# Two MLPs of a decoder trunk: the order of up-projection units and down-projection pairs

## Chip, core and metric

The kernel runs on one core of one Trainium2 chip. The metric is the device time of one execution in microseconds (us); lower is better. Three timed runs of the kernel before gave 1999.71, 2004.2 and 1998.16 us.

## What is computed

A decoder trunk of two layers over 256 positions, width 2048, all in float32. Layer 0 mixes with a gated short convolution, layer 1 with multi-head latent attention. Each is followed by an MLP with hidden width 8192, and every sub-layer by a post-norm. The change touches the two MLPs alone:

```python
def sq_relu_mlp(x, w1, w2):
    return jnp.square(jax.nn.relu(x @ w1)) @ w2

h = layer_norm(ALPHA * h + mix, ln_g[layer, 0], ln_b[layer, 0])
h = layer_norm(ALPHA * h + sq_relu_mlp(h, mlp_w1[layer], mlp_w2[layer]), ...)
```

w1 is 2048 x 8192 and w2 is 8192 x 2048 for each layer.

## The kernel before, in words

**Precision.** TensorE multiplies in a reduced float32 form. So each operand is split into a high part (a cast on ScalarE, L127) and the rest, the low part (a subtraction on VectorE, L128). A product is then three matmuls: high x high, high x low and low x high.

**Passes.** An MLP is done in NQ = 8 passes q over the hidden width. A pass makes QC = 8 hidden tiles of 128 columns and multiplies them at once with their rows of w2. Passes 1 to 6 are called FAST.

**Units.** One hidden tile is one unit of W1 (`products`, L288, calling `mm_run`, L221). A unit goes over 16 K tiles. For each it issues a matmul of 512 columns (`high`, L215: the weights' high part against x, high and low side by side) and one of 256 columns (`low`, L219). In the K tile numbered TURNED = 2 of the first unit of a pass the low matmul comes ahead of the high one: the tile is "turned". The sums go to one of four PSUM banks in turn. ScalarE copies half of them out (L355), VectorE adds the other half (L356), and ScalarE applies relu and square (L718, L719). Two hidden tiles make a pair; the pair is split and four sums and differences of its quarters are formed (`form`, L703).

**Products in pairs.** In a FAST pass the 2048 output columns are two groups g of 1024. Each group takes the four pairs j in turn. A "fast" pair (`fast_products`, L343) uses seven products for what needs eight, 21 matmuls of 512 columns (`dot`, L297), and seven PSUM sums named 1 to 7. Its weights come as two tiles of w2f, from which VectorE and ScalarE make the third and fourth matrix (`prepare`, L141). A "plain" pair uses eight products on four sums, 24 matmuls. Group 1 has three fast pairs and a plain one (MIXED = "sssp"), group 0 four fast ones. One matmul of the plain pair is split in two halves (EVEN, L654).

**Sums.** The sums of a pass are kept in SBUF: four in the output's own place `acc`, four extra ones in `sums`. At the end of a group they are copied back (`put_back`, L616) or added (`keep`, L624). Before the next pass's products they are copied into PSUM again (`resumed`, L612), for group 1 during the units of that pass. In the last pass `fold` (L669) combines the extra sums into `acc`.

**Order.** Everything follows the order in which the code is written and the order that the framework's scheduler gives each engine from it. In a FAST pass it is: eight units; four pairs of group 1; four pairs of group 0. Weights are taken from one list, `stream` (L78 to L99), in that order. `take` (L183) prepares a fixed number of steps ahead (LOOK = 5); five raw tiles (L62) and eight pairs of high and low tiles (L63) limit it. Loads are issued on SP (L138).

**Around it.** In the second MLP the residual is transposed on TensorE into `acc` during passes 1 to 4 (`extra`, L1024). In the first MLP chunks of the next norm are prepared in the last pass (`begin`, L798). In the last pass of the second MLP, sums are put into PSUM ahead of the output (`last_sum`, L681).

Of the kernel before, what the change touches and what calls it, by code (L numbers as in the profile page):

```python
# [16 lines left out]
P = 128  # L17
# [20 lines left out]
MIXED = "sssp"  # L38
EVEN = (QC - 1, "22")
# [14 lines left out]
def trunk(ctx: ExitStack, tc: tile.TileContext, xT, vecs, lead, w_first, w_in, w_out, w_kv, w_q, w_uk, w_uv,  # L54
# [27 lines left out]

    def mlp_stream(l):
        out = []
        for q in range(NQ):
            out += halves(w1[l, q * QC:(q + 1) * QC])
            if q not in FAST:
                out += halves(w2[l, q])
                continue
            for j, kind in enumerate(MIXED):  # L90
                out += [(w2f[l, q, 1, j, 0], w2f[l, q, 1, j, 1])] if kind == "s" else \
                    halves(w2[l, q, 2, j]) + halves(w2[l, q, 3, j])
            out += [(w2f[l, q, 0, j, 0], w2f[l, q, 0, j, 1]) for j in range(QC // 2)]
        return out
# [480 lines left out]
    def mlp(idx, ln, blocks, fast, begin=None, extra=None, last=False):  # L575
# [32 lines left out]
        def resumed(p, g, name, bank):  # L608

            ps = psum(name, bank)  # L610
            if q != FAST[0] or p not in OWN:
                nc.scalar.copy(ps, place(p, g))  # L612
            return ps

# [3 lines left out]
        def keep(p, g, ps):  # L618

            at = place(p, g)  # L620
            if q == FAST[0] and p in OWN:
                nc.scalar.copy(at, ps)
            else:
                nc.vector.tensor_tensor(at, at, ps, ALU.add)  # L624

        def resume(busy, free, ps, m):

            b2, b3, b4, b6 = free
            b1, b5, b7, b22 = busy
            for p, bank in {3: (("3", b3),), 4: (("2", b2),), 5: (("4", b4), ("1", b1)), 6: (("6", b6), ("5", b5)),  # L630
                            7: (("7", b7), ("22", b22))}.get(m, ()):
                ps[p] = resumed(p, 1, f"ps_r{p}", bank)

        def down_pairs(h, forms, busy, free, ps):

            b2, b3, b4, b6 = free
            b1, b5, b7, b22 = busy
            new = set(OWN) if q == FAST[0] else set()
            onto = set(ps) - new
            for j, kind in enumerate(MIXED):  # L640
                if kind == "s":
                    last = j == MIXED.rindex("s")
                    fast_products(ps, h, forms, j, new if j == 0 else (), OWN if last else (), onto)
                    if last:
                        for p in OWN:
                            put_back(p, 1, ps[p])
                        then = {p: resumed(p, 0, f"ps_f{p}", bank) for p, bank in (("3", b1), ("1", b5))}
                    continue
                for two in (((0, "2"), (1, "4")), ((1, "22"), (0, "3"))):
                    w, = take(1, LOOK + 1)  # L650
                    for t, p in two:
                        for kk in range(2):
                            k = 2 * j + kk
                            dot(ps[p], wide_rows(w, kk), held(h[k], t), False, k == QC - 1, (k, p) == EVEN, True)  # L654
                    if j == len(MIXED) - 1:
                        if "5" not in then:
                            then.update({p: resumed(p, 0, f"ps_f{p}", bank) for p, bank in (("5", b7), ("7", b6))})
                        for _, p in two:
                            put_back(p, 1, ps[p])
            n = QC // 2  # L660
            onto = set(then) - new
            then.update({p: psum(f"ps_f{p}", bank) for p, bank in (("2", b2), ("6", b4), ("4", b22))})
            for j in range(n):
                fast_products(then, h, forms, j, set(then) - onto if j == 0 else (), then if j == n - 1 else (), onto)
            for p, _, _ in FACTORS:
                (put_back if p in onto or p in new else keep)(p, 0, then[p])
            return (b3, b1, b5, b7), (b6, b2, b4, b22)

        def fold():  # L669

            s1, s5, s7, s6 = (sums[:, i] for i in range(4))
            c = acc.rearrange("p t (g b c) -> p t b g c", g=2, b=2)
            for d, a, b in ((c[:, 0, 0], c[:, 0, 0], s1), (s6, s6, s1), (c[:, 0, 1], c[:, 0, 1], s6), (s7, s7, s6),
                            (c[:, 1, 0], c[:, 1, 0], s7), (c[:, 1, 1], c[:, 1, 1], s7),
                            (c[:, 0, 1], c[:, 0, 1], s5), (c[:, 1, 1], c[:, 1, 1], s5)):
                nc.vector.tensor_tensor(d, a, b, ALU.add)
                yield
# [8 lines left out]
        busy, free = (0, 1, 2, 3), (4, 5, 6, 7)  # L686
        for q in range(NQ):
            ht = act.tile([P, QC, 2 * T], F32R, tag="c", name=f"h{idx}_{q}")
            h = [ht[:, k, :] for k in range(QC)]
            forms = None  # L690
            if q in FAST:
                forms = act.tile([P, QC // 2, 2, 4 * P], F32R, tag="a2", name=f"forms{idx}_{q}")
            pair = []

            def pair_tile(m):

                if m % 2 == 0:
                    pool = (act, "ab") if m % 4 else (fast, "fp")
                    t = pool[0].tile([P, 2 * T], F32, tag=pool[1], name="fp")
                    pair.append(t.rearrange("p (i t) -> p i t", i=2))  # L700
                return pair[-1]

            def form(j):  # L703
                (a11, a21), (a12, a22) = ((pair[j][:, i, :P], pair[j][:, i, P:]) for i in range(2))
                sf = fast.tile([P, 4, P], F32, tag="sf", name="sf")
                s1, s2, s3, s4 = (sf[:, i, :] for i in range(4))
                nc.vector.tensor_tensor(s1, a21, a22, ALU.add)
                nc.vector.tensor_tensor(s3, a21, a11, ALU.subtract)
                nc.vector.tensor_tensor(s2, s1, a11, ALU.subtract)
                nc.vector.tensor_tensor(s4, a12, s2, ALU.subtract)  # L710
                split(forms[:, j, 0, :], forms[:, j, 1, :], sf.rearrange("p i c -> p (i c)"))

            def hidden(m, ps, evac, *func):
                both = pair_tile(m) if q in FAST else None
                f = both[:, m % 2, :] if both is not None else tmp.tile([P, T], F32, tag="fh", name="fh", bufs=3)
                evac(ps, f, *func)
                if not func:
                    nc.scalar.activation(f, f, AF.Relu)  # L718
                nc.scalar.activation(f, f, AF.Square)  # L719
                if both is None:  # L720
                    put_split(h[m], f)
                elif m % 2:
                    at = ht[:, m - 1:m + 1, :]
                    split(at[:, :, :T], at[:, :, T:], both)
                    form(m // 2)

            if q == 0:
                for m in range(QC):
                    if m < GROUP:
                        if m == 0:  # L730
                            ws = ln.ws if ln.ws else group_of(GROUP)
                            if not ln.ws:
                                mm_wide(ws, ln.xd)
                            ln.finish()
                        ps = ws[m][1]
                    else:
                        ws = [(take(), psum("ps_w"))]
                        mm_wide(ws, ln.xd)
                        ps = ws[0][1]
                    hidden(m, ps, ln.weighted, AF.Relu)  # L740
                acc = act.tile([P, 2, D], F32, tag="a1", name=f"acc{idx}")
            else:
                folds = fold()
                begun = {}
                for m, ps in enumerate(products(QC, xhl, TURNED, busy)):
                    hidden(m, ps, whole)
                    if extra and m == 0 and q <= NB:
                        for t in range(2):
                            extra(block, q - 1, t, busy[2 + t])
                    if q in FAST:  # L750
                        resume(busy, free, begun, m)
                    if q == NQ - 1:
                        next(folds, None)
                        if last and m >= QC - 2:
                            for t in range(2):
                                last_sum(m - QC + 2, t, free[2 * (m - QC + 2) + t])
# [19 lines left out]
    def to_wide(block, put, h):  # L776
# [411 lines left out]
```

## Time and profile before

| what | value |
|---|---|
| timed runs, median (lowest to highest) | 1999.71 us (1998.16 to 2004.2) |
| span of the profiled execution, first to last instruction | 1994.9 us |
| from that span to the median of the timed runs | 4.8 us |
| VectorE's full-size split L128, count and mean | 710 of 1220 ns |
| ScalarE's full-size cast L127, count and mean | 710 of 1051 ns |
| HBM read | 381.78 MB, 192 GB/s over the span |

The profile is one execution on the chip; beside its span the page gives no device time of its own. Engines are PE (TensorE matmuls), PEld (TensorE's weight loads), DVE (VectorE), ACT (ScalarE), POOL (GpSimd) and SP. A row of grouped instructions reads: line, engine, operation, out<-in, shapes, count | busy us, mean ns | idle time before them and what ended it. A row of the timeline reads: start in us, duration in us, engine, line, operation. A matmul's duration reaches into the next one, so its cost is read from start to start. A row of the waits reads: who waited for whom, us in total, times, longest.

### The profile page before, as it was taken

How to read it: one execution, taken by the hardware profiler on the slowest of the kernel's cores; microseconds unless marked ns; L12 is line 12 of the kernel's file. 1: busy time of each engine (PE TensorE's matmuls, PEld its weight loads, DVE VectorE, ACT ScalarE, POOL GpSimd, SP SyncE). 2: the span in 40 equal slices, each digit the busy share in tenths (PEclk: the TensorE clock that was granted, in tenths of full speed). 3: DMA queues.
4: the chain of work that ended last, by engine and by line, in shares of the span. 5: the costliest groups of instructions: out<-in, count | busy, mean ns of one | idle time of the engine just before them, and what ended most of it. 6: DMA issues, size and time to landing. Idle time of an engine off the chain costs nothing.

```text
span 1994.9 us, 30180 instructions
## 1 busy us (share of the span) xinstructions
PE 1987.7 (100%) x11110; PEld 1737.2 (87%) x11110; DVE 1709.4 (86%) x2555; ACT 1354.9 (68%) x2154; POOL 2.3 (0%) x21
## 2 busy tenths in 40 slices
PE   9999999999999999999999999999999999999998
PEld 8888888988888888888889998898888888888886
DVE  8667667797999989989978988777899999999985
ACT  6444445586778778777756755558677787887772
POOL 0000000000000000000000000000000000000000
PEclk9999999999999999999999999999999999999999
DMA  8666666565657466574855543656464656656483
GB/s 318 205 191 187 190 190 190 179 193 157 212 170 251 148 216 221 177 243 147 281 171 159 170 140 123 201 180 195 146 233 155 232 161 220 222 178 233 150 269 130
DMA packets 106853, 385.85 MB, mean 193 GB/s; under 512 B 11857, under 2 KB 12625, under 8 KB 106449
## 3 DMA queue, kind: packets, MB, share of 16 engines
q1 hardware_dynamic: 106560, 383.79, 59.5%
q8 instruction: 87, 1.43, 0.3%
q14 instruction: 62, 0.50, 0.1%
q10 hardware_dynamic: 144, 0.13, 0.0%
HBM read 381.78 MB, written 2.10 MB: 192 GB/s over the span
## 4 chain that ended last, share of the span: by engine, by line
PE 98%; DVE 1%; ACT 1%; issue 0%; DVEq 0%; ACTq 0%
PE ps_u L215 20%; PE ps_l L215 13%; PE ps_u L219 10%; PE ps_l L219 7%; PE ps_f L300 4%; PE ps_f L303 4%; PE ps_f L302 4%; PE ps_r L303 4%; PE ps_r L302 4%; PE ps_r L300 4%; PE ps_d L300 2%; PE ps_d L302 2%; PE ps_d L303 2%; PE ps_w L249 2%; PE ps_w L248 2%; PE ps_w L247 2%
## 5 line engine op out<-in xcount | busy, mean ns | idle before, releaser
L128 DVE TENSOR_TENSOR lo<-raw,hi 128x1024 fp32r<-128x1024 f32 x710 | 861.8, 1220 | 190.6 <-ACT hi L127 119.9
L127 ACT CAST hi<-raw 128x1024 fp32r<-128x1024 f32 x710 | 741.8, 1051 | 247.4 <-PE ps_l L215 98.1
L215 PE MATMUL ps_u<-xhl,hi 128*128 128x512 f32 x1792 | 621.7, 392 | 0.0
L219 PE MATMUL ps_u<-xhl,lo 128*128 128x256 f32 x1792 | 498.2, 279 | 0.0
L215 PEld LDWEIGHTS ps_u<-xhl,hi 128*128 128x128 f32 x1792 | 334.5, 187 | 73.6 <-ACT acc L595 0.2
L219 PEld LDWEIGHTS ps_u<-xhl,lo 128*128 128x128 f32 x1792 | 338.1, 189 | 1.8
L215 PE MATMUL ps_l<-xhl_a,hi 128*128 128x512 f32 x704 | 244.1, 393 | 0.0
L219 PE MATMUL ps_l<-xhl_a,lo 128*128 128x256 f32 x704 | 195.4, 279 | 0.0
L215 PEld LDWEIGHTS ps_l<-xhl_a,hi 128*128 128x128 f32 x704 | 132.1, 188 | 29.9
L219 PEld LDWEIGHTS ps_l<-xhl_a,lo 128*128 128x128 f32 x704 | 131.9, 188 | 0.2
L127 ACT CAST hi_t<-raw_t 128x1024 fp32r<-128x1024 f32 x84 | 88.5, 1054 | 45.8 <-DVE raw_t L162 41.4
L162 DVE TENSOR_TENSOR raw_t<-raw,raw 128x1024 f32<-128x1024 f32 x84 | 102.3, 1218 | 1.8 <-DMA raw<-in_w2f_dram 1.5
L128 DVE TENSOR_TENSOR lo_t<-raw_t,hi_t 128x1024 fp32r<-128x1024 f32 x84 | 102.4, 1219 | 0.2
L718 ACT ACTIVATE fp<-fp 128x256 f32<-128x256 f32 x96 | 40.0, 416 | 63.2 <-DVE fp L356 62.6
L215 PE MATMUL ps_l<-z,hi 128*128 128x512 f32 x240 | 82.4, 391 | 0.0
L300 PE MATMUL ps_d<-hi,h 128*128 128x512 f32 x192 | 75.0, 391 | 0.0
L302 PE MATMUL ps_d<-lo,h 128*128 128x512 f32 x192 | 75.0, 390 | 0.0
L303 PE MATMUL ps_d<-hi,h 128*128 128x512 f32 x192 | 74.8, 389 | 0.0
L249 PE MATMUL ps_w<-xd,hi 128*128 128x258 f32 x256 | 72.7, 284 | 0.0
L248 PE MATMUL ps_w<-xd,lo 128*128 128x258 f32 x256 | 72.3, 282 | 0.0
L247 PE MATMUL ps_w<-xd,hi 128*128 128x258 f32 x256 | 72.3, 282 | 0.0
L215 PE MATMUL ps_l<-oT,hi 128*128 128x512 f32 x208 | 71.3, 391 | 0.0
(296 smaller groups left out, 3963.7 us busy)
## 6 DMA issues: line engine op xcount, KB each, us to landing
raw<-in_w_dram SPq DMA_DIRECT2D x344, 512.0 KB, 4.5
raw<-in_w2f_dram SPq DMA_DIRECT2D x168, 512.0 KB, 3.9
raw<-in_w_in_dram SPq DMA_DIRECT2D x88, 512.0 KB, 4.2
raw<-in_w_out_dram SPq DMA_DIRECT2D x32, 512.0 KB, 3.7
raw<-in_w_o_dram SPq DMA_DIRECT2D x32, 512.0 KB, 4.2
raw<-in_w_kv_dram SPq DMA_DIRECT2D x10, 512.0 KB, 3.7
raw<-in_w_q_dram SPq DMA_DIRECT2D x8, 512.0 KB, 4.0
raw<-in_w_uk_dram SPq DMA_DIRECT2D x8, 512.0 KB, 3.9
```

Of the source, the lines that this page charges most:

```text
L127: nc.scalar.copy(hi, src)
L128: nc.vector.tensor_tensor(lo, src, hi.bitcast(F32), ALU.subtract)
L162: nc.vector.tensor_tensor(t.rearrange(two, a=2), b12.unsqueeze(1).to_broadcast([P, 2, BW]), r1.rearrange(two, a=2), ALU.subtract)
L215: nc.tensor.matmul(ps, w[blk // 8][0][:, blk % 8, :], x, start=first, stop=False)
L219: nc.tensor.matmul(ps[:, :T], w[blk // 8][1][:, blk % 8, :], x[:, :T], start=False, stop=last)
L247: nc.tensor.matmul(ps[:, :W], hi, x[k][:, :W], start=k == 0, stop=False)
L248: nc.tensor.matmul(ps[:, :W], lo, x[k][:, :W], start=False, stop=False)
L249: nc.tensor.matmul(ps[:, :W], hi, x[k][:, W:], start=False, stop=k == NC - 1)
L300: nc.tensor.matmul(ps, x[0], w[0], start=first, stop=False, skip_group_check=onto)
L302: nc.tensor.matmul(ps[:, at], x[0], w[1][:, at], start=False, stop=False, skip_group_check=onto)
L303: nc.tensor.matmul(ps, x[1], w[0], start=False, stop=last, skip_group_check=onto)
L718: nc.scalar.activation(f, f, AF.Relu)
```

## The change

The eight units of a pass no longer stand together. A list of steps gives, for each unit of passes 1 to 7, the pair that follows it: unit m of pass q is followed by pair number m - 5 of pass q, or, for m under 5, by pair number m + 3 of pass q - 1. So three pairs of a pass stand among its own last units, and five among the first units of the next pass. The first five units and the last three of an MLP have no pair behind them.

The groups alternate: pass p takes group p % 2 first, then the other one. The second group of a pass is the first of the next, so its sums stay in PSUM. Only after the first group of a pass are sums copied back and those of the other group put into PSUM. The pass's one plain pair is now the last of its first group. VectorE's additions of sums (`keep`) are gone.

Units with a pair behind them all use one PSUM bank; the products use the seven others. Every unit has its turned K tile. The split of one matmul (EVEN) is gone. All hidden tiles and forms of passes 1 to 7 use one set of tiles, and a pair of hidden tiles is finished after its second unit's pair of products. `fold` works on one group at a time; the residual's transposes all stand in pass 1; `prepare_chunks` runs in the last three units and the first two downs.

```diff
-MIXED = "sssp"
-EVEN = (QC - 1, "22")
+PLAIN = tuple(FAST)
+SHIFT = 5
+def TURN(q, m):
+    return True
...
+    def steps():
+        for q in range(1, NQ):
+            for m in range(QC):
+                p, i = (q, m - SHIFT) if m >= SHIFT else (q - 1, m + QC - SHIFT)
+                yield q, m, (p, i // NB, i % NB, (p % 2) ^ (i // NB)) if p in FAST else None
+    def plain(q, i, j):
+        return i == 0 and j == NB - 1 and q in PLAIN
...
+        base = Banks.count
+        bank = {p: (base + i) % 8 for i, p in enumerate(("6", "unit", "3", "1", "5", "7", "2", "4"))}
...
+        def products_of(p, i, j, g):
+            order = [f[0] for f in FACTORS]
+            end = i == 0 or p == FAST[-1]
+            if plain(p, i, j):
+                for two in (((0, "2"), (1, "4")), ((1, "22"), (0, "3"))):
+                    w, = take(1, LOOK + 1)
+                    for t, o in two:
+                        for kk in range(2):
+                            dot(ps[o], wide_rows(w, kk), held(h[2 * j + kk], t), False, kk == 1, False, True)
+                for o in ("2", "4", "22", "3"):
+                    put_back(o, g, ps[o])
+                for o in ("3", "1", "2", "4"):
+                    resume(o, 1 - g)
...
+            own = i == 0 and j == NB - 2 and plain(p, 0, NB - 1)
+            fast_products(ps, h, forms, j, set(fresh), OWN if own else order if j == NB - 1 and end else (), onto)
+            if own:
+                for o in ("1", "5", "7", "6"):
+                    put_back(o, g, ps[o])
+                resume("22", g, "1")
+                for o in ("5", "7", "6"):
+                    resume(o, 1 - g)
...
+        for q, m, pair in steps():
+            lone = pair is None
...
+            w = take(2, LOOK + 1)
+            at = "6" if lone and m % 2 == 0 else "unit"
+            un = psum("ps_u", bank[at])
+            mm_run([(w, un)], xhl, 0, NC, NC, turned=TURNED if TURN(q, m) else None)
+            f = pair_tile(m)[:, m % 2, :]
+            whole(un, f)
+            nc.scalar.activation(f, f, AF.Relu)
+            nc.scalar.activation(f, f, AF.Square)
+            if extra and q == FAST[0] and m < NB:
+                for t in range(2):
+                    extra(block, m, t, spare[1 + (2 * m + t) % 3])
+            if q == NQ - 1:
+                for _ in range(3 if m >= SHIFT else 2):
+                    next(folds, None)
+                if begin and m >= SHIFT:
+                    begin(range(3 * (m - SHIFT) + 1, 3 * (m - SHIFT) + 4))
+            if pair:
+                products_of(*pair)
+            if m % 2:
+                finish_pair(m // 2)
...
         for n in range(NB):
             down(h, put, n)
+            if n < 2:
+                prepare_chunks(range(10 + 3 * n, 13 + 3 * n))
```

More of the change, by code (lines that the diff above doesn't have):

```diff
@@ L626, in resume @@
[L626 to L667, printed above, removed]
@@ L684, in last_sum @@
             nc.scalar.copy(finals[n, t], block(n, t))
[L686 to L690, printed above, removed]
-            if q in FAST:
[L692 to L737, printed above, removed]
@@ L741, in mlp @@
-                acc = act.tile([P, 2, D], F32, tag="a1", name=f"acc{idx}")
-            else:
[L743 to L756, printed above, removed]
-                        if begin:
-                            begin(range(max(2 * m, 1), 2 * m + 2))
@@ L760, in mlp @@
[L760 to L774 removed]
+                    ln.finish()
@@ new lines, in mlp, with resume @@
+        base = Banks.count
+        bank = {p: (base + i) % 8 for i, p in enumerate(("6", "unit", "3", "1", "5", "7", "2", "4"))}
+        spare = [bank[p] for p in ("3", "1", "5", "7", "2", "4", "6", "unit")]
+        forms = act.tile([P, QC // 2, 2, 4 * P], F32R, tag="a2", name=f"forms{idx}")
+        ps, onto, fresh = {}, set(), set()
+        folds = iter(())
+        def resume(p, g, at=None):
+            ps[p] = psum(f"ps_{p}", bank[at or p])
+            onto.discard(p)
+            if p in OWN and begun[g] == FAST[0]:
+                fresh.add(p)
+            else:
+                nc.scalar.copy(ps[p], place(p, g))
+                onto.add(p)
@@ L776, in to_wide @@
+        for _ in folds:
+            pass
+        if last:
+            for i, (n, t) in enumerate(((2, 0), (3, 0), (2, 1), (3, 1))):
+                last_sum(n, t, spare[4 + i])
+            blocks(block, finals, h)
+            return
+        Banks.count = base + 2
+        blocks(block, put, h)
     def to_wide(block, put, h):
@@ L796, in trunk, with prepare_chunks @@
     before, ln = ln, Norm(1, ALPHA)
-    def prepare_chunks(chunks):
+    def prepare_chunks(chunks, bank=None):
         for k in chunks:
-            ln.prepare(k, 0)
+            ln.prepare(k, bank)
     with tc.tile_pool(name="fast1", bufs=1) as fast:
```

117 lines of the change are left out of this document (74 added, 43 removed).

## The prediction

> **What bounds the kernel now.** I read the page first: the shares of the engines, then the chain of work that ended last.
>
> ```profile
> PE 1987.7 (100%) x11110; PEld 1737.2 (87%) x11110; DVE 1709.4 (86%) x2555; ACT 1354.9 (68%) x2154; POOL 2.3 (0%) x21
> PE 98%; DVE 1%; ACT 1%; issue 0%; DVEq 0%; ACTq 0%
> ```
>
> TensorE is never without a matmul and carries 98% of the chain, so the time is the sum of the steps from one matmul's start to the next. The view of waits, asked for the weight loads, lists all that TensorE waited for; these rows are the ones inside the two MLPs.
>
> ```profile
> PEld ps_f L300 <- ACT acc L616: 0.9, 1, 0.9
> PEld ps_f L300 <- ACT ps_f L612: 0.3, 1, 0.3
> PEld ps_d L300 <- DVE fh L356: 0.3, 1, 0.3
> PEld ps_u L215 <- ACT acc L595: 0.2, 1, 0.2
> ```
>
> So 1.7 us is all that smoother feeding could win back, and 0.3% of the time is 6.0 us. What the other engines are spared is worth nothing beyond that; what counts is how the matmul steps change and whether a new wait arises. The table of stretches shows how near that is. These are the units and the products of one pass, and the product stretch that holds the 0.9 us wait.
>
> ```profile
> core 0: us, PE busy (x) PEld busy (x) DVE busy (x) ACT busy (x) POOL busy (x), PEclk, DMA share, GB/s
> 702.50:746.90 44.40, 44.40 (x258) 39.13 (x257) 39.47 (x57) 34.20 (x56) 0.00 (x0) 1.00 0.61 210
> 746.90:785.70 38.80, 38.80 (x174) 32.11 (x174) 38.63 (x45) 31.20 (x47) 0.00 (x0) 1.00 0.57 181
> 913.30:953.00 39.70, 39.24 (x174) 31.97 (x173) 39.53 (x48) 32.16 (x48) 0.00 (x0) 1.00 0.54 177
> ```
>
> VectorE is busy 99% of the product stretch (38.63 of 38.80) and 89% of the units (39.47 of 44.40): it is the next bound. The granted clock is 1.00 throughout.
>
> **The matmul steps.** The timeline of TensorE over that pass, first columns start and duration, gives what a unit and a product cost in their present places.
>
> ```profile
> 702.46 0.39 PE L215 MATMUL ps_u<-xhl,hi 128*128 128x512 f32 x1
> 708.02 0.39 PE L215 MATMUL ps_u<-xhl,hi 128*128 128x512 f32 x1
> 746.85 0.39 PE L300 MATMUL ps_r<-hi,forms 128*128 128x512 f32 x1
> 748.93 0.39 PE L300 MATMUL ps_r<-hi_t,forms 128*128 128x512 f32 x1
> 766.64 0.39 PE L300 MATMUL ps_f<-hi,forms 128*128 128x512 f32 x1
> 785.68 0.39 PE L215 MATMUL ps_u<-xhl,hi 128*128 128x512 f32 x1
> ```
>
> - The first unit, the one with the turned K tile, takes 708.02 - 702.46 = 5.56; the seven after it (746.85 - 708.02) / 7 = 5.547 each. A turned unit behind products costs about 0.015 more than a unit behind a unit.
> - The 84 matmuls of the second group take 785.68 - 766.64 = 19.04, or 0.2267 each.
> - The first nine matmuls behind a unit (746.85 to 748.93) take 2.08 instead of 9 x 0.2267 = 2.04: each passage from unit to products costs 0.04.
> - The first group (19.79) has 86 whole matmuls and two halves, the split at L654. 87 x 0.2267 is 19.72; of the 0.07 left, 0.04 is the passage and 0.03 the split.
>
> **The change part by part**, per MLP, of which there are two.
>
> 1. *Units between pairs (products_of, steps).* Moved columns stay the same: 8 units, 7 pairs of 21 matmuls and one plain pair of 24 per pass. But 48 pairs now each follow a unit, and the last pass's down follows one: 49 passages instead of 7. 42 x 0.04 = +1.7 us. This is on the path: TensorE has nothing to hide it under.
> 2. *A turned K tile in every unit (TURN).* 49 units follow products instead of 7: 42 x 0.015 = +0.6. Seven turned units follow a unit (five at the head, two at the end). No row shows a turn inside a running stream of units. The nearest row below is 5.547, no cost; above it stands a unit that has no turn and runs badly, the one of the w_out product:
>
> ```profile
> 273.06 0.40 PE L215 MATMUL ps_u<-z,hi 128*128 128x512 f32 x1
> 278.71 0.40 PE L215 MATMUL ps_l<-z,hi 128*128 128x512 f32 x1
> ```
>
>    That is 5.65, 0.10 over. A gain is not excluded but would be under 0.1 too (sixteen pairs at the 0.34 of a first pair are 5.44). I take 0.02 each, near the turned row: +0.1; the ends are -0.7 and +0.7.
> 3. *The split at EVEN is gone.* 6 x 0.03 = -0.2.
> 4. *Sums stay in PSUM over passes.* In a middle pass eight of ScalarE's PSUM copies (L612, L616) at 0.58 each and three VectorE adds go; sixteen half-size folds replace eight. On the path only where TensorE waited: the 0.9 and 0.3 above, -1.2 in all over both MLPs.
> 5. *prepare_chunks is spread* over three units and two downs: the same short VectorE instructions beside TensorE, no cost as long as VectorE keeps up there. If it didn't, six of them would be late in to_wide, at 0.42 each, 2.5 us at the most. The rows of the copies and of these:
>
> ```profile
> L612 ACT COPY ps_r<-acc 128x512 f32<-128x512 f32 x48 | 27.8, 583 | 0.1
> L616 ACT COPY sums<-ps_r 128x512 f32<-128x512 f32 x48 | 25.6, 586 | 23.2 <-PE ps_r L303 23.2
> L415 DVE SCALAR_TENSOR_TENSOR xres<-xres,mu 128x256 f32<-128x256 f32 x45 | 16.6, 418 | 0.0
> ```
>
>    DMA issues on SP keep their number and size, four to a step of unit and pair.
> 6. *One bank for the units.* Before, four banks took turns, so a unit's sums had three units to be read out. Now the next unit waits for the add of L356 into the same bank, with one pair (21 x 0.2267 = 4.76) in between. What stands before that add on VectorE follows from its rows, start to start:
>
> ```profile
> 811.97 0.42 DVE L356 TENSOR_TENSOR fp<-ps_u,t 128x256 f32<-128x256 f32 x1
> 812.30 0.68 DVE L166 TENSOR_TENSOR raw<-raw,raw_t 128x512 f32<-128x512 f32 x1
> 812.90 1.22 DVE L128 TENSOR_TENSOR lo<-raw,hi 128x1024 fp32r<-128x1024 f32 x1
> 814.03 0.28 DVE L707 TENSOR_TENSOR sf<-fp 128x128 f32<-128x128 f32 x1
> 814.24 0.69 DVE L169 TENSOR_TENSOR raw<-raw 128x512 f32<-128x512 f32 x1
> ```
>
>    An add takes 0.33, a half-size step 0.60, a full one 1.13, a quarter 0.21. A step has two splits for the unit (2.26), the add (0.33), four full and three half-size steps for the pair (6.32) and half of a tile pair's finish (four quarters, two halves: 1.02): 9.9 us, while TensorE needs 5.56 + 4.76 + 0.04 = 10.36. VectorE fills 96% of a fast step and 5.9 of the plain one's 11.0, so some 75 of a pass's 83.5 (now 78). The bulk fits. In the built program's order the add of a unit stands behind at most one split whose buffer is freed by the same unit's end. Its cast, from this row of ScalarE, is 1.05, then the copy 0.36, the split 1.13 and the add 0.33:
>
> ```profile
> L127 ACT CAST hi<-raw 128x1024 fp32r<-128x1024 f32 x710 | 741.8, 1051 | 247.4 <-PE ps_l L215 98.1 <-DMA raw<-in_w_dram 29.9 <-PE ps_d L303 27.9
> L355 ACT COPY t<-ps_u 128x256 f32<-128x256 f32 x112 | 40.4, 361 | 0.0
> raw<-in_w2f_dram SPq DMA_DIRECT2D x168, 512.0 KB, 3.9
> ```
>
>    Together some 2.7 us after the unit's end, against 4.76: I take no wait, with 2 us to spare. Behind the add on VectorE stand the next weights' splits, which TensorE wants a whole step (10.4) later. A raw tile's transfer (3.9) starts when the third-matrix split ends, about 5 us before ScalarE wants it, 1 us to spare.
>
> Sum: +1.7 + 0.6 + 0.1 - 0.2 = +2.2 per MLP, +4.4 for two, less 1.2: about **+3.2 us**. The span goes from 1994.9 to about 1998. The timed runs have a median of 1999.71, 4.8 above the span of the profiled execution, and I keep that distance: **2003**. The plain step's group switch, where ScalarE has eight copies of 0.58 and two casts ahead of the first bank that TensorE wants again, fits too: 6.8 us of work in the 11.0 between the start of the plain pair and the next pair.
>
> A rule that speaks against pricing order at all: the Trainium skill ("TensorE: Matmul & The Clock Gate", Back-to-back issue gap) gives an isolated step of N/2.4 + 2.5 ns, whatever stands before. The rows above disagree in size (227 ns for 512 columns where it gives 216) and show that order matters (0.04 a passage). By it items 1 to 3 would fall out of the sum, which would be -1.2.
>
> **The rivals.**
>
> - *Late evacuation (slower).* Place: the add of L356 into the one unit bank, or a split that the plain step's copies push back. It decides when the add comes more than 4.76 after the unit's end, 2 us later than I count. For it: VectorE at 96% of a fast step, and the 0.9 us wait in a stretch where it stood at 99%. Against: twelve such stretches gave one wait of note; each plain step gives 5 us back. Price: 84 fast steps, each late by 0.1 to 0.3, are 8 to 25 us: 2012 to 2029, 2014 likeliest. Chance 0.27.
> - *The turn doesn't take behind an odd run.* All runs of products ahead of a turned unit are now even in number (172 or 192 matmuls); a fast pair has 21. If the bad rhythm of the 273.06 unit then holds in half of the 48 units, 24 x 2 x 0.09 = +4.3: 2007.8; in all of them 2012. For it: no row shows an odd run. Against: after nine matmuls the steps are back at 0.227 whatever came before. Chance 0.22.
> - *Order costs nothing.* Only the waits go: 1998.5. Against it stand the 0.04 and 0.015. Chance 0.06.
> - *Relief (faster).* All waits go and the turned units run better than 5.547: every turned unit at 5.50 would be 112 x 0.05 = 5.6 less, and even that with the 1.2 only just passes 0.3%: 1993. Nothing shows such a unit. Chance 0.03. That the order isn't as described is excluded: the built program has one unit ahead of each pair.
>
> **How the numbers follow.** My forecast has the chance that is left, 0.42, with a range of its own of 2001 to 2006. The whole range takes in the bottom of the order-free case and most of the late evacuation: 1998.5 to 2018. A measurement of this kernel can tell about 0.3% from no change, 1993.7 to 2005.7. Within it: nearly all of the forecast (0.39), the order-free case, and 0.02 of the odd runs: 0.47. Slower: 0.27 + 0.20 + 0.03 = 0.50. Faster: 0.03.
>
> **What would show it.** Right: TensorE still near 100%, no wait of ps_u on L367 (the add's new line) beyond 1 us in sum, turned units of 5.56, pairs of 21 matmuls of 4.80, passes of about 83.6 between like matmuls, L128 fewer waits for ScalarE. Odd runs: units alternating between 5.56 and 5.65. Late evacuation: a row of PEld ps_u waiting for DVE fp, or of products waiting for lo, tens of times. Wrong at the root would be a unit well under 5.5 or pairs away from 0.227 a matmul.

## The result, and the profile after

The changed kernel takes 2003.3 us (median of 12 runs, 2001.67 to 2004.89). The kernel before took 1999.74 in the same rounds (12 runs, 1996.41 to 2004.2). The ratio is 1.0019, with a 95% interval of 1.0011 to 1.0027: slower by 3.6 us. The prediction was 2003.0.

In the profiled executions the distance is twice as large: the span went from 1994.9 to 2002.0, +7.1. Both numbers are real, and why they differ is part of what follows. The page of the profile after, its engines and its chain:

```profile
PE 1994.1 (100%) x11098; PEld 1738.4 (87%) x11098; DVE 1687.5 (84%) x2529; ACT 1313.3 (66%) x2074; POOL 2.3 (0%) x21
PE 89%; DVE 5%; DMA 3%; issue 2%; ACT 1%; DVEq 0%; ACTq 0%
```

TensorE is still never short of a matmul for long, but its part of the chain fell from 98% to 89%, and VectorE and the DMAs have entered it. The waits after name two rows that matter, one of TensorE's weight loads and one of VectorE:

```profile
PEld ps_u L226 <- DVE fp L367: 3.2, 6, 1.2
DVE raw_t L173 <- DMA raw<-in_w2f_dram: 42.9, 36, 2.8
```

The first is the unit's bank waiting for VectorE's add. The second is VectorE waiting for the tiles of w2f; in the same view of the kernel before it was small:

```profile
DVE raw_t L162 <- DMA raw<-in_w2f_dram: 1.5, 5, 0.6
```

The timeline of TensorE after, starts in the first column, from the head of the first MLP into its first steps:

```profile
453.11 0.39 PE L226 MATMUL ps_u<-xhl,hi 128*128 128x512 f32 x1
486.92 0.40 PE L311 MATMUL ps<-hi,forms 128*128 128x512 f32 x1
...
502.07 0.39 PE L226 MATMUL ps_u<-xhl,hi 128*128 128x512 f32 x1
507.63 0.39 PE L311 MATMUL ps<-hi,forms 128*128 128x512 f32 x1
512.44 0.39 PE L226 MATMUL ps_u<-xhl,hi 128*128 128x512 f32 x1
518.00 0.39 PE L311 MATMUL ps<-hi,h 128*128 128x512 f32 x1
523.48 0.39 PE L226 MATMUL ps_u<-xhl,hi 128*128 128x512 f32 x1
```

- A fast step is 512.44 - 502.07 = 10.37: a unit of 5.56 and 21 products in 4.81. A plain step is 11.04. That is what was forecast.
- The six units at the head take 33.81, or 5.635 each. Turned units that follow a unit were priced at 5.567.
- All 96 units that follow a pair take 5.56 or 5.57, apart from six that had to wait for the add (5.59, and five of 5.67 to 5.76).

The late adds show in VectorE's timeline around one of these waits (in brackets the idle time before, and what ended it):

```profile
1677.67 0.42 DVE L367 TENSOR_TENSOR fp<-ps_u,t 128x256 f32<-128x256 f32 x1
...
1679.74 3.49 DVE L139 TENSOR_TENSOR lo<-raw,hi 128x1024 fp32r<-128x1024 f32 x3
1684.36 1.23 DVE L173 TENSOR_TENSOR raw_t<-raw,raw 128x1024 f32<-128x1024 f32 x1 [1.13 <-DMA raw<-in_w2f_dram]
...
1688.17 0.42 DVE L367 TENSOR_TENSOR fp<-ps_u,t 128x256 f32<-128x256 f32 x1
...
1694.90 1.22 DVE L173 TENSOR_TENSOR raw_t<-raw,raw 128x1024 f32<-128x1024 f32 x1
...
1700.18 0.42 DVE L367 TENSOR_TENSOR fp<-ps_u,t 128x256 f32<-128x256 f32 x1
```

and TensorE's at the same place:

```profile
1694.93 0.39 PE L311 MATMUL ps<-hi,forms 128*128 128x512 f32 x1
...
1700.65 0.50 PE L226 MATMUL ps_u<-xhl,hi 128*128 128x512 f32 x1 [0.75 <-DVE fp L367]
```

VectorE stands 1.13 us for a transfer at 1683.23. It then works almost without a gap (20.49 of the 21 us from 1684 on), and at the second add behind the stop it is still late: the unit ends at 1694.93, its add starts at 1700.18, 5.25 later, and the next unit starts 0.92 late (5.72 behind the pair's first matmul instead of 4.80). The chain shows the transfer that VectorE stood for:

```profile
1678.00 1.23 DVE lo L139
...
1679.25 5.02 DMA raw<-in_w2f_dram
```

It started when the subtraction of a low part (L139) had freed its tile, 4.0 us before VectorE wanted it, and took 5.0.

Where the 7.1 us of the two profiled executions come from, by the starts of the matmuls:

| part | us | read from |
|---|---|---|
| units between pairs, one K tile turned behind products | +4.7 | runs e5 and e11 below, 2.3 to 2.4 per MLP |
| turned K tiles in units that follow a unit | +0.9 | first MLP 0.7: 33.81 and 16.85 against 33.30 and 16.66 in run e1; second MLP 0.2: 36.95 and 16.85 against 36.91 and 16.66 in run e11 |
| waits for the add, and units that run badly behind them | +2.4 | 1.7 in the pairs, 0.7 in six units |
| a wait of the kernel before that is gone | -0.9 | products of 19.97 instead of 19.04 at 933.1 |
| start, and between the MLPs | 0.0 | +0.33 and -0.3 |

The sum is 7.1 of 7.1.

### The profile page after: what moved, and what is told of

The parts are those of the page before. It is cut to its first block, busy times and chain, and to the rows that moved or that the text cites. A ratio compares the mean times of both kernels' runs of the same rounds, so it can differ in the third digit from the quotient of the medians.

```text
span 2002.0 us, 30028 instructions
## 1 busy us (share of the span) xinstructions
PE 1994.1 (100%) x11098; PEld 1738.4 (87%) x11098; DVE 1687.5 (84%) x2529; ACT 1313.3 (66%) x2074; POOL 2.3 (0%) x21
## 4 chain that ended last, share of the span: by engine, by line
PE 89%; DVE 5%; DMA 3%; issue 2%; ACT 1%; DVEq 0%; ACTq 0%
PE ps_u L226 17%; PE ps_l L226 13%; PE ps_u L230 9%; PE ps_l L230 7%; PE ps L313 6%; PE ps L314 6%; PE ps L311 6%; DMA raw<-in_w2f_dram 2%; PE ps_d L313 2%; PE ps_d L314 2%; PE ps_d L311 2%; DVE lo L139 2%; PE ps_w L260 2%; PE ps_w L259 2%; PE ps_w L258 2%
## 5 line engine op out<-in xcount | busy, mean ns | idle before, releaser
L139 DVE TENSOR_TENSOR lo<-raw,hi 128x1024 fp32r<-128x1024 f32 x710 | 857.2, 1220 | 177.4 <-ACT hi L138 102.1
L230 PE MATMUL ps_u<-xhl,lo 128*128 128x256 f32 x1792 | 483.8, 280 | 0.0
L226 PEld LDWEIGHTS ps_u<-xhl,hi 128*128 128x128 f32 x1792 | 328.3, 187 | 68.7 <-DVE fp L367 3.2
L173 DVE TENSOR_TENSOR raw_t<-raw,raw 128x1024 f32<-128x1024 f32 x84 | 102.6, 1222 | 43.8 <-DMA raw<-in_w2f_dram 42.9
L314 PE MATMUL ps<-hi,h 128*128 128x512 f32 x264 | 103.6, 392 | 0.0
L313 PE MATMUL ps<-lo,h 128*128 128x512 f32 x264 | 103.2, 391 | 0.0
L139 DVE TENSOR_TENSOR lo_t<-raw_t,hi_t 128x1024 fp32r<-128x1024 f32 x84 | 102.4, 1219 | 0.4 <-ACT hi_t L138 0.4
L311 PE MATMUL ps<-hi,h 128*128 128x512 f32 x264 | 102.6, 388 | 0.0
```

The costliest lines, as they stand in the source:

```text
L139: nc.vector.tensor_tensor(lo, src, hi.bitcast(F32), ALU.subtract)
L173: nc.vector.tensor_tensor(t.rearrange(two, a=2), b12.unsqueeze(1).to_broadcast([P, 2, BW]), r1.rearrange(two, a=2), ALU.subtract)
L226: nc.tensor.matmul(ps, w[blk // 8][0][:, blk % 8, :], x, start=first, stop=False)
L230: nc.tensor.matmul(ps[:, :T], w[blk // 8][1][:, blk % 8, :], x[:, :T], start=False, stop=last)
L311: nc.tensor.matmul(ps, x[0], w[0], start=first, stop=False, skip_group_check=onto)
L313: nc.tensor.matmul(ps[:, at], x[0], w[1][:, at], start=False, stop=False, skip_group_check=onto)
```

## The experiments

Theory on the first point: what TensorE pays is set by the order of its matmuls, and the turned K tile gives a unit its good pace (5.55 to 5.57 us) only right behind products. A rival is that the place of the turn is worth nothing. Theory on the second point: the waits come from VectorE standing before late transfers; the rival is that VectorE is simply full.

### The order of the matmuls

**e1: the turn only in units behind products.**

```diff
 def TURN(q, m):
-    return True
+    return not (q == 1 and 1 <= m <= SHIFT or q == NQ - 1 and m > SHIFT)
```

> The changed kernel, but the 14 units that follow another unit keep the plain order of their K tiles; the 98 behind products stay turned. Rhythm theory (a turn inside a running stream of units costs 0.085 us, read as 33.81 us for the six units at the head of the first MLP against 6 x 5.565): those units fall from 5.65 to 5.55, 14 x 0.09 = 1.2 us less than the changed kernel, about 2002, ratio to the kernel before about 1.0012. Rival, the late evacuation is the whole loss: no change beyond noise, ratio 1.0019, units at the head still 5.65.

Measured: 2001.84 us (11 runs), ratio 1.0019 (1.0010 to 1.0028). Starts in TensorE's timeline, head of the first MLP:

```profile
452.82 0.39 PE L226 MATMUL ps_u<-xhl,hi 128*128 128x512 f32 x1
486.12 0.39 PE L311 MATMUL ps<-hi,forms 128*128 128x512 f32 x1
```

The six units take 33.30 instead of 33.81: each of the five that follow a unit lost 0.10 by its turn. The step is shown, but the time as a whole did not come down against the kernel before. The profiled execution, at 2003.94 us the longest of the eleven, has more waits for the add (4.5 us in the weight loads' row, nine times) than the changed kernel's (3.2, six).

**e2: no turn at all.** `TURN` returns False.

> The changed kernel without any turned K tile. Rhythm theory: a unit behind products falls into the bad rhythm of the w_out product's unit (5.65 instead of 5.565), 98 x 0.09 = 8 to 9 us more, about 2011. Rival, the turn is worth nothing behind short runs of products: units of 5.55, 98 x 0.015 = 1.5 us less than the changed kernel, about 2002.

Measured: 2007.78 us (4 runs), ratio 1.0046 (1.0032 to 1.0059). A step in TensorE's timeline:

```profile
491.72 0.39 PE L226 MATMUL ps_u<-xhl,hi 128*128 128x512 f32 x1
497.36 0.40 PE L311 MATMUL ps<-hi,forms 128*128 128x512 f32 x1
502.15 0.39 PE L226 MATMUL ps_u<-xhl,hi 128*128 128x512 f32 x1
```

A unit behind products takes 5.64, 0.075 more than with the turn; for 96 of them that is 7.2 us. The span grew by only 4.0 over the changed kernel's (2006.0). Behind such a unit a pair takes 4.787 instead of 4.802, which is 1.4 less in all. And the slower steps leave VectorE time: the waits for the add fall to 0.7 us, some 1.8 less with the units behind them. So the order of the matmuls decides, and a slower TensorE is paid back in part.

**e3: the kernel before, a turn in every unit.**

```diff
-            mm_run([(w, ps)], x, 0, NC, NC, turned=None if i else turned)
+            mm_run([(w, ps)], x, 0, NC, NC, turned=turned)
```

> The kernel before with one part of the change alone: a turned K tile in every unit, the units still in eights. Rhythm theory: the 98 units that follow a unit go from 5.547 to 5.65, about 8 to 10 us more, ratio about 1.0045. Rival, a turn in a running stream costs as little as behind products (0.018): 1.8 us more, ratio 1.001.

Measured: 2005.89 us (4 runs), ratio 1.0037 (1.0023 to 1.0051). The eight units of a pass, from the first unit to the first product:

```profile
452.99 0.39 PE L215 MATMUL ps_u<-xhl,hi 128*128 128x512 f32 x1
498.10 0.40 PE L300 MATMUL ps_r<-hi,forms 128*128 128x512 f32 x1
```

45.11 instead of 44.39 (44.40 in the prediction's table): 0.72 for seven turns that follow a unit, 0.10 each, the same as in e1. One turn starts a good run, and the next one ends it.

**e6: the kernel before without the split matmul.**

```diff
-EVEN = (QC - 1, "22")
+EVEN = None
```

> The kernel before without the split of one matmul per pass (the split at EVEN). Theory (the split is worth only its own 0.03 us): product groups of 87 and 84 matmuls, 0.03 us less per fast pass, 12 passes: -0.4 us in the span, turned units behind them still 5.57 and the seven after them 5.547. Rival (an odd run of products breaks the rhythm of the units behind it): eight units at 5.64, 12 x 8 x 0.09 = +8.6 us.

Measured: 1998.04 us (one run). The starts of the first group of products, of the second and of the unit behind them, in TensorE's timeline:

```profile
497.18 0.39 PE L300 MATMUL ps_r<-hi,forms 128*128 128x512 f32 x1
...
516.94 0.39 PE L300 MATMUL ps_f<-hi,forms 128*128 128x512 f32 x1
...
535.98 0.39 PE L215 MATMUL ps_u<-xhl,hi 128*128 128x512 f32 x1
```

The first group takes 19.76, 0.03 less than with the split, and so it does in all twelve passes. The second takes 19.04 as before wherever it does not wait, and the units behind are as before. So the split cost 0.03 a pass, as item 3 had it, and the odd run of 87 matmuls breaks no rhythm. The time did not show it, because this execution has more waits of products for ScalarE's copies than both profiles of the kernel before:

```profile
PEld ps_f L300 <- ACT acc L616: 2.8, 5, 0.9
```

They stretch six of the twelve second groups by 2.6 us in all, and the span is 1996.2, 1.6 over that of e5 below.

### The plain pair

**e4: e1 without plain pairs**, so that each pair has seven products (21 matmuls in place of 24, more splits for VectorE).

```diff
-PLAIN = tuple(FAST)
+PLAIN = ()
```

> The version of e1 with the plain pair of each pass made a fast one: 12 x 3 x 0.2267 = 8.2 us of matmuls less. If VectorE still keeps up (8 x 9.9 = 79 us of a pass of 82.9), the time is about 1994, ratio 0.997. If the plain step is what lets VectorE catch up, the fast steps become late evacuations one after another: waits of ps_u for L367 in the tens of us, and the time is 2000 or more.

Measured: 2019.4 us (4 runs), ratio 1.0105 (1.0092 to 1.0119), although TensorE has 36 matmuls less, 36 x 0.2267 = 8.2 us. The waits of the weight loads:

```profile
PEld ps L311 <- ACT forms L138: 13.7, 12, 1.8
PEld ps L313 <- DVE lo L139: 10.6, 9, 1.6
PEld ps L314 <- DVE forms L139: 2.5, 6, 0.8
PEld ps_u L226 <- DVE fp L367: 0.9, 4, 0.4
```

and one of VectorE:

```profile
DVE raw_t L173 <- DMA raw<-in_w2f_dram: 41.8, 17, 4.3
```

The row that the expectation named, the unit's bank waiting for the add, has 0.9 us and not tens. The loss lies at the group switch, once in each pass. The last pair of the first group, no longer plain, now needs forms, and the last hidden tiles' forms are finished only one step before: that is the first row. Behind it ScalarE has 14 copies of sums to make (seven out, seven in) where the plain step has eight. Its casts come behind them, VectorE stands up to 4.3 us for a transfer, and the next pair waits for its splits: the second row. Counted from unit to unit against 10.37, the four steps from the pair that was plain on lose 25.8 us in all, the other four of each pass 2.6. So e4 does not show that fast steps which fill VectorE to 96% fail. Whether VectorE could keep up without any relief stays open, since the waits at the switch also give it time. What the run shows is what else the plain pair does: it needs no forms, and it lets the sums be changed in two steps.

1.7 of the 25.8 us come from the clock. At the switch of pass 2 TensorE pauses twice within 2.5 us, for 1.4 and for 0.5 us by the starts of its matmuls; behind that the matmuls start 0.43 apart for some 3.4 us instead of 0.23. The timeline of TensorE, and the row of the table of stretches for two us behind it (the clock is the third figure from the end):

```profile
601.98 0.50 PE L311 MATMUL ps<-hi,forms 128*128 128x512 f32 x1 [1.26 <-ACT forms L138]
...
603.07 0.67 PE L314 MATMUL ps<-hi,forms 128*128 128x512 f32 x1 [0.36 <-DVE forms L139]
...
604.00:606.00 2.00, 2.00 (x6) 0.50 0.20 80
```

### What lies between the span and the time

**e5: the kernel before, unchanged**, for a second profile.

> The kernel before, unchanged, for a second profile. Theory (waits that vary): the steps of the matmuls are fixed and what differs between executions is how long TensorE waits for VectorE and ScalarE; a profile whose span lies x above 1994.9 should show about x more in waits of the products or units and in units that run badly behind a wait, and units of 44.39 and products of 38.83 a pass everywhere else. Time minus span stays at 1.8. Rival (the clock or the start varies): the same waits as in the first profile (1.7 in the MLPs) and the difference elsewhere.

Measured: 1996.39 us with a span of 1994.6, against 1998.46 as the median of 19 runs of the kernel before on that chip (1996.86 to 2002.1). So this execution was a quick one again, and a profile of a long one of this very kernel was not to be had. The nearest is e6, the kernel before but for 0.4 us: 1.6 us longer in span, and 2.6 us of waits. What e5 does show is that 1.8 us lie around the span, not 4.8; the profiled execution of the changed kernel has the same 1.8 (2003.81 and 2002.0). It also gives the kernel before free of waits, from the first unit of an MLP to what follows the last:

```profile
453.35 0.39 PE L215 MATMUL ps_u<-xhl,hi 128*128 128x512 f32 x1
997.10 0.39 PE L300 MATMUL ps_d<-hi,h 128*128 128x512 f32 x1
...
1394.20 0.50 PE L215 MATMUL ps_u<-xhl,hi 128*128 128x512 f32 x1
1941.48 0.39 PE L300 MATMUL ps_e<-hi,h 128*128 128x512 f32 x1
```

543.75 and 547.28.

### More room for the transfers

**e7 and e8: seven raw tiles and seven pairs of split tiles**, in the kernel before and in e1.

```diff
-RAW, WA = 5, 8
+RAW, WA = 7, 7
```

> The kernel before with seven raw tiles and seven pairs of split tiles in place of five and eight. Theory (a raw tile freed late makes its transfer late, VectorE stands behind it, and TensorE then waits): transfers start earlier, the waits that vary between executions go, and the median comes down to the least seen, about 1996.7: ratio 0.9985. Rival (the split tiles were the scarcer ones): TensorE waits for lo, slower by some us: ratio 1.002 or more. If the transfers don't matter here: 1.000.

> The changed kernel with its turned K tile only in units behind products, and with seven raw tiles and seven pairs of split tiles in place of five and eight. Theory (VectorE waits some 49 us in all for transfers of the third matrix, and the add into the unit bank stands behind these waits): VectorE's wait on the transfers falls under 10 us, TensorE's waits for the add (4.5 us) go, and the units that ran badly behind them too (1.5): median about 2001.8 - 5 = 1997, ratio 0.999 against the kernel before. Rival (the add is late because VectorE is full, not because it waits): the transfers' waits go but the waits for the add stay: ratio 1.0015 to 1.002. Rival (the split tiles were the scarcer ones): TensorE waits for lo, ratio over 1.003.

Measured: e7 1997.67 us (10 runs, 1996.76 to 1999.36), ratio 0.9993 (0.9984 to 1.0003). Its runs lie closer together than those of the kernel before beside them (1996.86 to 2002.1), but the medians cannot be told apart. e8 2002.57 us (10 runs), ratio 1.0016 (1.0007 to 1.0025). In e8 VectorE has no wait for a transfer of w2f and TensorE none for the add; both MLPs run at their steps' own pace. Yet the time did not fall: the end, from the first matmul of the last products to the start of the kernel's last matmul, takes 50.90 instead of 48.41. The expectation did not foresee that. TensorE's timeline shows the pause before the last eight matmuls:

```profile
1988.77 0.39 PE L314 MATMUL ps_e<-hi,h 128*128 128x512 f32 x1
1991.30 0.96 PE L1084 MATMUL ps_e<-gbt,umeans 128*128 128x512 f32 x1 [2.14 <-ACT umeans L1082]
```

and the table of stretches what follows it (the last columns are the granted clock, the DMA share and GB/s):

```profile
core 0: us, PE busy (x), PEclk, DMA share, GB/s
1992.00:1994.00 2.00, 2.00 (x4) 0.50 0.02 7
```

The last eight matmuls start at half the clock and take 4.8 us from the first start to the last (1991.30 to 1996.10) instead of 3.1 (in e1 1994.35 to 1997.46). That is 1.7 of the 2.5 us. The other 0.8 is the later start: in e7, whose last eight matmuls ran at the full clock, the end takes 49.20.

**e9 and e10: six raw tiles, seven pairs of split tiles** (`RAW, WA = 6, 7`), in e1 and in the kernel before, in the same rounds.

> The changed kernel with its turned K tile only in units behind products, six raw tiles and seven pairs of split tiles (five and eight in the change; seven and seven in the run before it). Theory (TensorE's waits for the add come from VectorE standing before late transfers, and one more raw tile is enough to end that): no waits for the add, both MLPs as with seven raw tiles (546.1 and 549.7 us). The end behind the second MLP took 50.9 there instead of 48.4; if the seven pairs of split tiles do that (the last weights are split late), it stays near 50.9 and the ratio at 1.0016; if the seven raw tiles did, it is 48.4 and the ratio 1.0005.

> The kernel before with six raw tiles and seven pairs of split tiles, on the chip and in the rounds of the changed kernel with the same buffers. Theory (both then free of waits, so what is left between them is the matmuls' order): MLPs of 543.75 and 547.3, and a time 2 x 2.35 = 4.7 us under that of the changed kernel with the same buffers, ratio about 0.9985 to 0.9995 against the kernel before. Rival (the order isn't it, the buffers are): less than 2 us between the two.

Measured: e9 2002.58 us, ratio 1.0014 (1.0005 to 1.0023); e10 1999.23 us, ratio 0.9999 (0.9990 to 1.0008), 11 runs each. e9 has both MLPs at 546.07 and 549.68, as with seven raw tiles, and an end of 50.89, so the seven pairs of split tiles cost the end, not the raw tiles. e10 lies 3.4 us under e9, less than the 4.7 expected and more than the rival's 2: its own products still wait (544.26 and 548.18 in the two MLPs, 0.5 and 0.9 over e5).

**e11 and e12: six raw tiles, eight pairs, one T4 buffer** (the weights of the seventh product) in place of two, which frees the room.

```diff
-RAW, WA = 5, 8
+RAW, WA = 6, 8
...
-        f = state["fast"].tile([P, 2, BW], F32R, tag="t4", name=f"t4_{i}", bufs=2)
+        f = state["fast"].tile([P, 2, BW], F32R, tag="t4", name=f"t4_{i}", bufs=1)
```

> The changed kernel with its turned K tile only in units behind products, six raw tiles, all eight pairs of split tiles, and one buffer in place of two for the seventh factor's weights (T4). Theory: with eight pairs the end takes 48.4 again, and with six raw tiles the waits for the add go: 1998.3 to 2000, ratio 1.0005 to 1.001. Rival (the one T4 buffer blocks VectorE's queue: it is read last in a pair, so the next split into it stands until the pair ends): TensorE waits for T4 or for the add in many pairs, 5 us or more, ratio 1.003 or more.

> The kernel before with six raw tiles, eight pairs of split tiles and one T4 buffer. Here pairs follow each other within 4.76 us, so the next T4 has to be split within one pair. Theory (waits that vary go with the late transfers, the end stays at 48.4): 1996.5 to 1997.5, ratio 0.999. Rival (the one T4 buffer blocks VectorE's queue): TensorE waits for T4 in the pairs, 84 x 0.1 us or more, ratio 1.004 or more.

Measured: e11 2000.54 us (11 runs, 1999.63 to 2001.13), ratio 1.0003 (0.9994 to 1.0012); e12 1998.99 us (11 runs, 1997.11 to 2000.42), ratio 0.9994 (0.9986 to 1.0003). The end of e11 takes 48.41 again, and the time lies 0.5 above the expected range. e12 lies only 1.6 us under e11, and 1.5 above its own range. Its median is 1.1 above its own profiled execution, and there the second MLP takes 548.50, 1.2 over e5: two products wait 0.6 us for splits into T4, and the eight units behind one of these waits run at 5.63 to 5.66 instead of some 5.55. So e12 is no measure of the kernel before without waits. e5 is. The MLPs of e11, in TensorE's timeline:

```profile
452.61 0.39 PE L226 MATMUL ps_u<-xhl,hi 128*128 128x512 f32 x1
998.68 0.39 PE L311 MATMUL ps_d<-hi,h 128*128 128x512 f32 x1
...
1395.51 0.39 PE L226 MATMUL ps_u<-xhl,hi 128*128 128x512 f32 x1
1945.18 0.39 PE L311 MATMUL ps_e<-hi,h 128*128 128x512 f32 x1
```

546.07 and 549.67, against 543.75 and 547.28 in e5: 2.32 and 2.39 us are what the new order of the matmuls costs, the missing split included. VectorE's wait for the transfers is down from 49.0 us in e1 to this row:

```profile
DVE raw_t L173 <- DMA raw<-in_w2f_dram: 10.3, 23, 1.2
```

How the adds moved is read from the starts of all 96 of them, behind the end of their unit. The next unit starts 4.80 behind that end if nothing is late; an add takes 0.42, so one that starts more than 4.3 behind is too late or nearly so.

| kernel | median | latest | over 4.3 |
|---|---|---|---|
| the changed kernel | 2.67 | 5.25 | 5 |
| e1 | 2.92 | 5.00 | 9 |
| e4, no plain pair | 2.88 | 6.91 | 17 |
| e11, six raw tiles and eight pairs | 2.17 | 3.55 | 0 |
| e8, seven raw tiles | 2.31 | 2.35 | 0 |

VectorE has the same work in e1, e8, e9 and e11, and its adds come in time wherever its waits for transfers are short or gone. So it is not too full for the add, and the rival falls. One thing more differs: with other numbers of buffers the scheduler also gives VectorE another order. In e9 only 8 of some 110 stretches between two adds hold the same instructions in the same order as in e1, while e1 and the changed kernel agree in all. By the work that stands ahead of them, the order favours five of e1's nine late adds in e9, by one full-size step (1.13 us); they come 2.7 to 3.3 earlier. The other four have as much or 0.5 more ahead of them, and still come 2.0 to 2.8 earlier. So the better part of it is that VectorE no longer stands before a transfer, and the order has a share in five of the nine.

No kernel was measurably under the kernel before. e12 and e7 come nearest, with intervals that take in 1.

## Why the prediction was right, and where it was not

The time came out at 2003.3 for 2003.0, inside the forecast's own range of 2001 to 2006. It is right in the price of the order. That it came within 0.3 us is luck: two of its steps erred by about as much in opposite directions.

- **Units between pairs, and the turn behind products (items 1 and 2).** Right. 42 passages and 42 turns were priced at 2.3 us per MLP, less 0.2 for the split; e11 against e5 shows 2.3 to 2.4 with the split gone. The passages cost their 0.04; a turned unit costs 0.018 more than a unit behind a unit (5.565 against 5.547) and not 0.015, 0.8 instead of 0.6 for 42. Pairs of 4.80, units of 5.56 and passes of 83.64 came as named.
- **Seven turned units that follow a unit (item 2).** Mis-sized: taken at 0.02 each, "near the turned row", they cost 0.10 (e1, e3). The bound from the badly running unit of the w_out product was the right row. It makes 0.7 in the first MLP in place of 0.1. In the second it makes only 0.2: there transposes stand between the units of the head, and units behind them run badly without a turn too (5.63 to 5.74 in e11).
- **The split (item 3).** Right: 0.03 a pass (e6).
- **Waits of before (item 4).** They did go, but they were worth 0.9 and not 1.2: by the starts of the matmuls the two waits, 0.9 and 0.3 in the weight loads' rows, had cost 0.93 together. In the timed runs there was probably more of them than the profile showed; see below.
- **One bank (item 6): "I take no wait, with 2 us to spare".** This step failed, in its tail. The sum of some 2.7 us to the end of the add (its terms add up to 2.9) is near the median: 2.67 to its start, 3.0 to its end. It failed where it took each raw tile's transfer to be in time, "1 us to spare": 3.9 us for the transfer and a start 5 us ahead. In the stretch shown above it was 5.0 and 4.0. VectorE waited for these transfers 36 times, 42.9 us in all, with about 0.5 us of spare time in a fast step (10.36 - 9.9) to make good for it. So TensorE waited six times, 2.4 us in all with the units behind. The rival "late evacuation" had the mechanism, but took it to hit all 84 fast steps (8 to 25 us, which on 2003.0 give 2011 to 2028 and not 2012 to 2029). No run shows that: e4's loss lies at the group switch.
- **The distance from span to median, 4.8.** This step failed as well. 1.8 us lie around the span. The other 3.0 were the distance of the profiled execution of the kernel before from its own median. Added to the span of the changed kernel, they were counted as if they stayed: 1998 + 4.8. The changed kernel's span came out at 2002.0, 4.0 over its forecast, and its median lies 1.3 over that span instead of 4.8, 3.5 under. The two errors nearly cancel. What the 3.0 consists of was not seen in a profile of this kernel. That it is mostly waits is argued from four things: e6 is longer than e5 and waits more, with more raw tiles the runs of the kernel before spread less (e7), with slower units hardly at all (e3, 2005.58 to 2006.45 in four runs), and the matmul steps are the same in both of its profiles.
- **The rivals.** Odd runs: none of the 96 units shows it (the 2007.8 for it should be 2007.3, 2003.0 + 4.3). Order costs nothing: the place of one K tile moved the spans by 4 to 9 us (e2, e3). By the step of N/2.4 + 2.5 ns that the Trainium skill gives for an isolated matmul ("TensorE: Matmul & The Clock Gate", Back-to-back issue gap), which asks for nothing but the number of columns, e2 and e3 should not have moved at all; the measurement decides. Relief in the turned units: none below 5.56.

## What to carry to other kernels

Price an order of matmuls by rows in which the same neighbours stand, and where a trick is moved to a place that no row shows, take the price of the row that shows it absent or failing, not of the one where it works. A wait that was ruled out by a sum of durations needs the same check for every transfer in front of it: an engine at 96% makes good only a few tenths of a us per step. Compare the profiled execution's own time with the timed runs before adding any distance: one profile can be a quick execution, whose waits need not be those of the median. And when more buffers help, look whether they changed the order of the instructions too.

## What the runs showed of the hardware

- **Two paces of the same 32 matmuls.** A unit of alternating 512 and 256 columns takes 5.55 or 5.64 us with the same instructions. A turned K tile right behind products gives the good pace (5.565 against 5.64 in e2), one inside a good run ends it (0.10 a unit, e1 and e3), and behind a wait of TensorE a unit also runs badly: 5.67 to 5.76 in five places of the changed kernel. So a wait of 0.02 to 0.9 us there costs 0.1 to 0.2 more than itself. The bad pace lasts as long as units follow units: in e12 a wait of 0.1 us, two matmuls ahead of the first of eight units, is followed by eight at 5.63 to 5.66, 0.8 us in all. In the changed kernel the unit behind the next pair runs well again. Why the order sets the pace, no run shows.
- **The granted clock falls after a pause of 2.3 us, but not each time.** In the profiled executions of e8, e9 and e10 the last eight matmuls came 2.3 us behind the end of the ones before (start to start less 0.23 for the last of them), and the clock stood at 0.50 under about five of them. In e7 the pause was as long, and they ran at 1.00. The runs of e8 and e9 fall into two kinds: with a mean granted clock of 1.000 over the execution 2001.0 to 2001.7 us, with 0.999 2002.5 to 2003.0. Single pauses of 1.7 us in e1 and the kernel before left the clock at 1.00. In e4 two shorter ones in a row were once enough (1.4 and 0.5 us, the rows above), while later single ones of up to 1.5 us left the clock at 1.00. The Trainium skill ("TensorE: Matmul & The Clock Gate", Part 1: The HAM clock gate) gives an idle window of about 3.4 us as what brings half clock, in a window that runs freely; here 2.3 us were at times enough, and once less.
- **What lies around the span isn't quite fixed:** 1.7 to 1.9 us in most runs, but up to 2.2 in those of e7, 2.1 to 2.2 in those of e10 and 1.9 to 2.4 in those of e12 (the profiled one 1997.94 with a span of 1995.5). All three are the kernel before with other numbers of buffers; why, no run shows.
